# Low parts of the SwiGLU weight operands: a vector subtraction each, or a negation and an accumulating DMA each

## The chip, the cores and the metric

One core of a Trainium2 chip runs the kernel. The metric is device time in microseconds (us). The kernel before took 918.5 us (median of 3 runs, 917.46 to 919.3).

The engines are named as in the profile: PE (TensorE, matrix products; PEld is its loading of weights), DVE (VectorE), ACT (ScalarE), POOL (GpSimd) and SP (SyncE, which here only starts DMAs). Each works through its own queue in order.

## The reference

One layer of an encoder over 768 tokens (512 of a sample, 256 of a prompt), 1024 wide. A mixing block comes first (gated MLP, differential attention, neighbourhood attention), then a layer norm, then SwiGLU, then a layer norm. The change lies in the SwiGLU, whose inner width is 2816:

```python
def swiglu(x, w_gate, w_up, w_down):
    return (jax.nn.silu(x @ w_gate) * (x @ w_up)) @ w_down

def trunk(x, ...):
    ...
        x = layer_norm(DEEPNORM_ALPHA * x + mix, ln_g[l, 0], ln_b[l, 0])
        x = layer_norm(DEEPNORM_ALPHA * x + swiglu(x, w_gate[l], w_up[l], w_down[l]), ln_g[l, 1], ln_b[l, 1])
```

All of it is in float32.

## The kernel before

**Split products.** Every operand of a large product is split into two fp32r parts: `hi` is the value rounded to fp32r, `lo` is what the rounding lost. A product a b is then the sum of hi hi, hi lo and lo hi, three matmuls. Line 113 is the helper: ACT casts (line 114), and then DVE or POOL subtracts (line 115).

```python
def split(hi, lo, src, eng=V):
    S.copy(out=hi, in_=src)
    eng.tensor_tensor(out=lo, in0=src, in1=hi.bitcast(F32), op=ALU.subtract)
```

**The SwiGLU (from about 400 us on).** The inner width is worked through in 11 pairs p of 128-wide feature tiles. A weight of a pair is a 2 x 2 arrangement of blocks, and the block product is taken in seven products instead of eight (Strassen's scheme in Winograd's form), in the order 1, 2, 6, 5, 7, 3, 4. Pair 0 uses eight plain products, and the last two pairs of the down projection use four operands each. Each product has one weight operand of 128 x 512 numbers; there are 219 of them: 8 for pair 0, 140 for gate and up of pairs 1 to 10, 63 for the down projection of pairs 0 to 8, and 8 at the end. A product of gate or up is 12 matmuls 384 columns wide, one of the down projection 9 matmuls 512 columns wide.

For p = 1 to 9 the loop at line 1119 makes seven products of gate, four of the down projection of the pair before, seven of up, and the last three of that down projection: 21 operands. This is called a round below.

**How a weight operand is made.** SP loads a weight subchunk (128 x 1024) into one of 3 `raw` buffers (line 122); an operand group (gate, up or down of a pair) takes two subchunks. Products 1 and 2 use their blocks as loaded. For product 6 POOL forms sums of blocks (line 169), in place of blocks that are no longer needed: a block can be overwritten only when its own split is over. `ws` is one extra buffer for a sum; line 181 fills it again for product 7 of the down projection. Then line 179 splits the operand into a `w` tile; five such tiles hold two operands each, and one is free again when PE has used it. A raw buffer is free for the next load when the last operand made from it has been split: after product 3 (or 5, for the down projection) for the first subchunk of a group and after product 4 for the second.

Line 179 sets who subtracts: POOL for the first 6 operands and for products u3, u4 and d2 later on (`POOL_FIRST`, `POOL_LO`), 34 in all, and DVE for the other 185.

**The other work of a round.** PE's results lie in PSUM banks. ACT copies intermediate sums out (`snap`, line 1018); DVE adds them up (`ffs`, `bv`, line 1023), applies the gate (lines 934 and 937) and adds the down projection into `y` (line 1045). POOL forms sums of the gated blocks (lines 946 to 950), and ACT and DVE split those into `mix`. PE cannot overwrite a bank before DVE or ACT has read it.

**What sets the order.** PE's order is written out by the kernel. The order on ACT, DVE and POOL is worked out by the scheduler of the language from its own timing model; `tc.issue_after` (line 219) only lets the making of new operands in after a given instruction. A DMA that POOL starts stands in POOL's queue like its other instructions.

Of the kernel before, what the change touches and what calls it, by code (L numbers as in the profile page):

```python
# [10 lines left out]
ALU = mybir.AluOpType  # L11
# [3 lines left out]
P = 128  # L15
T = 768          # sample tokens 0..511, prompt tokens 512..767
NS = 512
D = 1024
KT = D // P      # 8
NT = T // P      # 6  # L20
FF = 2816
NFF = FF // P    # 22
# [4 lines left out]
H2 = T // 2      # 384  # L27
NP = NFF // 2    # 11 pairs of feature tiles in the SwiGLU
NP_ST = 9        # pairs whose down projection takes seven block products
PRODUCTS = (1, 2, 6, 5, 7, 3, 4)    # the order of the block products  # L30
OUT_ORDER = [6, 7, 2, 3, 4, 0, 1, 5]    # contraction order of the output projection

# where the smaller parts join the large products, on the clock that these make
CV_LAG = (2.59, 3.84)        # after v of C: its transposes
C_START = 7.75             # attention C: start, period of each pair of heads,
C_PERIOD = (3.18, 6.33)     # stages of a unit in periods
C_AT = (0, 1.03, 1.71, 2.0)
B_START = 61.0            # attention B: the same, and each head's lag after its k
# [3 lines left out]
A_AT = [(7.88, 3.48), (9.39, 3.47), (8.72, 2.82)]    # gMLP: mixing, then transposes  # L42
X1_LAG = (11.34, 9.57, 10.27, 10.2, 8.52, 12.18)    # transposes after the first norm
# how the work of the splits and of the last norm is shared out
POOL_FIRST = 6              # operands of the SwiGLU split with the help of Pool: the first ones,
POOL_LO = ("u3", "u4", "d2")    # and these later on
AHEAD = {"g": 2, "u": 2, "d": 0}    # splits let in by an operand's release
LAST_V = 768                # columns of the last token tile that the vector engine finishes, in two parts
WARM = 8                    # products on zeros before the first ones
LEAD = 2                    # final pieces whose first half runs ahead  # L50
# weight subchunks in the order of use, each [128, 1024]
# [8 lines left out]
def encoder_layer(ctx: ExitStack, tc, a, o):  # L60
# [17 lines left out]
    # The tensor engine keeps the order of emission: `main` holds the large products, whose time  # L78
    # is the clock; everything else is queued on that clock with `later`.
# [23 lines left out]
    # Items 0 .. W_FF - 1 are whole subchunks; from there on an item is a block operand of the  # L103
    # SwiGLU (half a subchunk wide), two of them to a tile.
# [8 lines left out]
    def split(hi, lo, src, eng=V):  # L113
        S.copy(out=hi, in_=src)  # L114
        eng.tensor_tensor(out=lo, in0=src, in1=hi.bitcast(F32), op=ALU.subtract)  # L115

# [26 lines left out]
    def ff_operand(n):  # L143
# [11 lines left out]
        else:  # L155
            if prod == 6:
                # the sums of blocks, in place of blocks no longer needed
                w_sum[key] = s1 = wk2.tile([P, 512], F32, tag="ws", name="ws", bufs=2)
                if down:
                    steps = ((s1, r[0][:, second], r[0][:, first], ALU.subtract),  # L160
                             (r[0][:, first], r[1][:, second], s1, ALU.subtract),
                             (r[1][:, first], r[1][:, first], r[0][:, first], ALU.subtract))
                else:
                    steps = ((s1, r[1][:, first], r[1][:, second], ALU.add),
                             (r[1][:, first], r[0][:, first], r[1][:, first], ALU.subtract),
                             (r[0][:, first], s1, r[0][:, first], ALU.subtract),
                             (r[0][:, second], r[0][:, second], r[0][:, first], ALU.subtract))
                for out, in0, in1, f in steps:
                    G.tensor_tensor(out=out, in0=in0, in1=in1, op=f)  # L169
# [9 lines left out]
        split(op[:, 0], op[:, 1], src, G if n < POOL_FIRST or (n > 16 and key[0] + str(prod) in POOL_LO) else V)  # L179
# [82 lines left out]
    # the tensor engine warms up on zeros while the first loads are under way  # L262
# [64 lines left out]
    # qs[:, m]: the head's own 64 partitions hold q_hi, the other 64 q_lo;  # L327
    # kk[:, m]: k_hi on both halves;  kl: k_lo, head m on its own 64 partitions.
# [52 lines left out]
    for h in range(4):  # L381
# [21 lines left out]
        # sample: first column block, inner column blocks, last column block; prompt: both  # L403
# [8 lines left out]
    def proj_nat(w0, evac):  # L412
        """token-major output, 256 columns: steps of one token tile and two contraction tiles"""
# [19 lines left out]
    def proj_T(wi0, x_hi, x_lo, done):  # L433
        """feature-major output of one 128-wide feature tile, [128, 768]: steps of one contraction tile"""
        st = {}

        def step(k):
            if k == 0:
                st["ps"] = (ps_mm(), ps_mm()[:, :T - NS])
            ps = st["ps"]  # L440
            w = w_tiles[wi0]
            sl = slice(k * P, (k + 1) * P)
            for wi, x in ((0, x_hi), (0, x_lo), (1, x_hi)):
                for p, c0, c1 in ((ps[0], 0, NS), (ps[1], NS, T)):
                    TE.matmul(p, lhsT=w[:, wi, sl], rhs=x[:, k, c0:c1],  # L445
                              start=(k == 0 and wi == 0 and x is x_hi), stop=(k == KT - 1 and wi == 1))
            if k == KT - 1:
                done(ps)
                w_done(wi0)

        return [(0.97, lambda k=k: step(k)) for k in range(KT)]

    def merge(p, q):
        """two lists of steps, evenly mixed"""
# [3 lines left out]
    def chain(stages, at):  # L458
        """stage s of a unit goes at[s] after its start"""
# [6 lines left out]
    def stream(units, period, at, gate=None):  # L466
        """units one period apart; a unit may have to wait for its gate"""
# [20 lines left out]
    cv = mxp.tile([P, NT, 256], F32, tag="mx", name="cv")  # L488

    def c_unit(pr, t):  # L490
# [35 lines left out]
        def values():  # L526
            # out^T, the two heads on their halves of the partitions
# [146 lines left out]
    def a_steps(w0, done):  # L674
        """gelu in stages, for a token tile of u or v"""
        def unit(t, ps):
            u = {}

            def first():
                u["xh"] = xh = wkp.tile([P, 256], F32, tag="xh", name="xh", bufs=2)  # L680
                u["tt"] = tt = wkp.tile([P, 256], F32, tag="tt", name="tt", bufs=2)
                # tanh argument: x * (c + c * 0.044715 * x^2) with x = 2 * xh
# [115 lines left out]
    # x1^T in blocks: 11, 21 the contraction halves of tokens 0..383, 12, 22 those of tokens  # L798
    # 384..767; t1 = 12 - 11, t2 = 22 - t1, t3 = 22 - 12, t4 = 21 - t2.
# [108 lines left out]
    # Products of 2 x 2 blocks take seven block products (Strassen, in Winograd's form): with  # L908
    # s1 = a21 + a22, s2 = s1 - a11, s3 = a11 - a21, s4 = a12 - s2 and t1 .. t4 as above,
    # p1 = a11 b11, p2 = a12 b21, p3 = s4 b22, p4 = a22 t4, p5 = s1 t1, p6 = s2 t2, p7 = s3 t3;  # L910
    # c11 = p1 + p2, c12 = p1 + p6 + p5 + p3, c21 = p1 + p6 + p7 + p4, c22 = p1 + p6 + p7 + p5.
    # One bank gathers p1, p6, p7, p4 and another p2, then p5, p3.
# [18 lines left out]
    def silu(i, src):  # L931
        # silu(x) = x / 2 * (1 + tanh(x / 2))
# [3 lines left out]
    def gated(i, src, p):  # L936
# [4 lines left out]
        # the down projection's blocks: 11, 12 (token, feature halves), their sums, 22  # L941
# [20 lines left out]
    def first_pair():  # L962
        """pair 0 by eight block products: tokens 384 .. 767 come last, their blocks as 11 + t1 and 22"""
        st = {}

        def step(kind, prod, k):
            f, part = prod // 10 - 1, prod % 10      # a f1 b11, a f2 b21, a f1 t1, a f2 b22
# [87 lines left out]
    def piece(i, p):  # L1055
        # part of a token tile, the last two pairs of feature tiles
# [20 lines left out]
    def finish(t, bn):  # L1077
# [4 lines left out]
        # the last steps of the tile before come after the statistics of this one  # L1082
# [60 lines left out]
def _ff_items():  # L1143
    """the weight operands of the SwiGLU in the order of use, and their subchunks in the order of loading"""
# [18 lines left out]
def _layout(inputs):  # L1163
    """Host side: layout only, and constants of the shapes."""
# [8 lines left out]
    def kblocks(w, kt):  # L1173
        # [1024, n] -> subchunks of kt contraction tiles: [128, kt * n]
# [75 lines left out]
```

## Time and profile before

| | |
|---|---|
| median of the runs | 918.5 us (917.46 to 919.3) |
| span of the profiled execution | 916.2 us |
| median of the runs less that span | 2.3 us |
| PE busy | 858.7 us, 94% of the span |
| DVE busy | 702.7 us, 77% |
| ACT busy | 423.2 us, 46% |
| POOL busy | 388.3 us, 42% |

The times of this profile are those of one execution; a run's time also holds a little that lies around the span. Busy shares are means over stages that differ: from 440 us to 820 us DVE is busy some 90% of the time and POOL half of it. A line of the code can be that of a helper: line 115 is every subtraction of a split, so the names of the tiles say which (`w` a weight, `mix` the activations). A wait is put down to what ended it.

### The profile page before, as it was taken

To read this page: it belongs to the slowest core of one execution; us is meant where nothing else is said; L and a number is where in the kernel's file an instruction comes from. 1 tells how busy PE (TensorE), PEld (TensorE's weight loads), DVE (VectorE), ACT (ScalarE), POOL (GpSimd) and SP (SyncE) were. 2 spreads that over 40 slices of the span, in tenths; PEclk is the share of its full clock that TensorE was granted. 3 is DMA by queue.
4 is the path that set the end of the run, shared out by engine and by line. 5 is a ranking of instruction groups with operands and counts; after the bars stand their busy time and mean duration, and the time that the engine had idled before them with its cause. 6 is when DMAs were issued, how large, how long until landed. Compare 5 with 4: busy or idle time off the path is not lost.

```text
span 916.2 us, 13012 instructions
## 1 busy us (share of the span) xinstructions
PE 858.7 (94%) x4811; PEld 761.0 (83%) x4811; DVE 702.7 (77%) x1217; ACT 423.2 (46%) x922; POOL 388.3 (42%) x323
## 2 busy tenths in 40 slices
PE   7999999999999998988999898999899989999995
PEld 6888898888987887887888797888888878879984
DVE  3563437675677569789989898989899898989678
ACT  3474467686665436543434343333334343424422
POOL 0570010100120048885555555554554555653126
PEclk9999999999999999999999999999999999999998
DMA  6830201111017202012222220212222112222223
GB/s 216 246 102 24 69 25 53 40 47 35 15 61 260 70 1 69 23 47 70 69 69 70 69 70 24 92 47 70 69 69 70 69 47 70 69 69 70 70 71 113
DMA packets 22304, 66.66 MB, mean 73 GB/s; under 512 B 3680, under 2 KB 5984, under 8 KB 22240
## 3 DMA queue, kind: packets, MB, share of 16 engines
q1 hardware_dynamic: 22240, 65.82, 21.8%
q8 instruction: 38, 0.62, 0.3%
q14 instruction: 26, 0.21, 0.1%
HBM read 62.67 MB, written 3.15 MB: 72 GB/s over the span
## 4 chain that ended last, share of the span: by engine, by line
PE 50%; DVE 29%; issue 6%; POOL 6%; DMA 5%; ACT 3%; SPq 0%; DVEq 0%; ACTq 0%; POOLq 0%
PE ff L1007 13%; DVE w L115 11%; PE mm L445 9%; PE mm L424 7%; DVE y L1045 6%; PE mm L840 5%; DVE mix L115 5%; PE sc L1040 2%; DVE ffs L934 2%; PE av L608 2%; DMA raw<-in_xT 2%; PE ff L1040 2%; ACT w L114 1%; DMA raw<-in_w 1%; POOL mix L115 1%
## 5 line engine op out<-in xcount | busy, mean ns | idle before, releaser
L115 DVE TENSOR_TENSOR w<-raw,w 128x512 fp32r<-128x512 f32 (+2 forms) x179 | 175.2, 998 | 30.0 <-ACT w L114 29.9
L114 ACT CAST w<-raw 128x512 fp32r<-128x512 f32 (+2 forms) x213 | 137.8, 675 | 105.8 <-PE ff L1007 34.3
L1007 PE MATMUL ff<-x,w 128*128 128x384 f32 x720 | 132.4, 336 | 1.5 <-DVE bv L992 1.5
L1007 PEld LDWEIGHTS ff<-x,w 128*128 128x128 f32 x720 | 126.3, 188 | 3.4 <-DVE bv L992 1.9
L1007 PE MATMUL ff<-xt,w 128*128 128x384 f32 x480 | 90.9, 341 | 13.5 <-DVE ffs L1023 13.5
L1007 PEld LDWEIGHTS ff<-xt,w 128*128 128x128 f32 x480 | 84.6, 190 | 16.4 <-DVE ffs L1023 16.4
L1007 PE MATMUL ff<-mix,w 128*128 128x384 f32 x480 | 92.6, 341 | 3.7 <-DVE bv L1023 2.7
L1007 PEld LDWEIGHTS ff<-mix,w 128*128 128x128 f32 x480 | 86.1, 192 | 5.3 <-DVE bv L1023 4.0
L445 PE MATMUL mm<-xhi,w 128*128 128x512 f32 x320 | 79.1, 346 | 0.5 <-DVE qs L342 0.5
L169 POOL TENSOR_TENSOR ws<-raw 128x512 f32<-128x512 f32 x29 | 41.7, 1440 | 80.4 <-DMA raw<-in_w 66.7
L169 POOL TENSOR_TENSOR raw<-raw 128x512 f32<-128x512 f32 x49 | 70.8, 1446 | 6.8 <-DVE w L115 3.5
L424 PE MATMUL mm<-w,xhi 128*128 128x256 f32 x384 | 71.4, 286 | 0.0
L840 PE MATMUL mm<-w,mix 128*128 128x512 f32 x270 | 68.3, 399 | 1.5 <-ACT tt L684 0.8
L1040 PE MATMUL ff<-w,mix 128*128 128x512 f32 x216 | 59.3, 404 | 10.8 <-DVE y L1045 10.6
L619 POOL TENSOR_TENSOR mn<-mn,neghalf 128x1 f32<-128x1 f32 x24 | 13.7, 572 | 116.2 <-DVE mn L618 112.3
L1018 ACT COPY snap<-ff 128x384 f32<-128x384 f32 x60 | 28.6, 477 | 70.7 <-PE ff L1007 70.7
L840 PEld LDWEIGHTS mm<-w,mix 128*128 128x128 f32 x270 | 49.2, 188 | 12.6 <-ACT tt L684 1.3
L424 PEld LDWEIGHTS mm<-w,xhi 128*128 128x128 f32 x384 | 58.1, 189 | 1.4 <-issue 0.9
L115 POOL TENSOR_TENSOR w<-raw,w 128x512 fp32r<-128x512 f32 x34 | 52.2, 1550 | 16.8 <-ACT w L114 16.6
L1040 PEld LDWEIGHTS ff<-w,mix 128*128 128x128 f32 x216 | 39.1, 189 | 23.8 <-DVE y L1045 17.5
L1040 PE MATMUL sc<-w,mix 128*128 128x512 f32 x189 | 51.8, 407 | 5.0 <-DVE y L1045 5.0
L445 PEld LDWEIGHTS mm<-xhi,w 128*128 128x128 f32 x320 | 49.1, 189 | 6.9 <-issue 0.8
(232 smaller groups left out, 1786.9 us busy)
## 6 DMA issues: line engine op xcount, KB each, us to landing
raw<-in_w SPq DMA_DIRECT2D x95, 512.0 KB, 3.4
y<-in_x SPq DMA_DIRECT2D x6, 512.0 KB, 8.7
raw<-in_xT SPq DMA_DIRECT2D x7, 384.0 KB, 5.0
out_y<-y SPq DMA_DIRECT2D x10, 256.0 KB, 2.0
ln<-in_lng SPq DMA_DIRECT2D x2, 512.0 KB, 6.9
ln<-in_lnb SPq DMA_DIRECT2D x2, 512.0 KB, 8.0
rpb<-in_rpbs SPq DMA_DIRECT2D x32, 30.6 KB, 3.4
rpb<-in_rpbp SPq DMA_DIRECT2D x16, 59.6 KB, 3.0
```

Of the source, the lines that this page charges most:

```text
L114: S.copy(out=hi, in_=src)
L115: eng.tensor_tensor(out=lo, in0=src, in1=hi.bitcast(F32), op=ALU.subtract)
L169: G.tensor_tensor(out=out, in0=in0, in1=in1, op=f)
L424: TE.matmul(ps, lhsT=x[:, k, t * P:(t + 1) * P], rhs=w[:, wi, sl], start=(k == 0 and x is xhi and wi == 0), stop=(k == KT - 1 and x is xlo))
L445: TE.matmul(p, lhsT=w[:, wi, sl], rhs=x[:, k, c0:c1], start=(k == 0 and wi == 0 and x is x_hi), stop=(k == KT - 1 and wi == 1))
L608: TE.matmul(av, lhsT=pT[:, b * P:(b + 1) * P], rhs=vt[:, j0 + b, c0:c0 + P], start=(b == 0), stop=(b == nb - 1))
L840: TE.matmul(ps, lhsT=mix[OUT_ORDER[i]][:, m, t * P:(t + 1) * P], rhs=w[:, wi, sl], start=(i == first and m == 0 and wi == 0), stop=(i == l ...
L934: V.scalar_tensor_tensor(out=TH[i], in0=TT, scalar=1.0, in1=src, op0=ALU.add, op1=ALU.mult)
L1007: TE.matmul(b, lhsT=w[:, wi, k * P:(k + 1) * P], rhs=x1_block(x_name[prod], m, k), start=(prod in (1, 2, 5) and k == 0 and wi == 0 and m = ...
L1018: S.copy(out=t, in_=st[2 if prod == 5 else 1])
L1040: TE.matmul(b, lhsT=gt_block(a_slot[prod], m)[:, t * P:(t + 1) * P], rhs=w[:, wi], start=(prod in (1, 2, 5) and m == 0 and wi == 0), stop= ...
L1045: V.tensor_tensor(out=y[t + dt][:, c], in0=b, in1=y[t + dt][:, c], op=ALU.add)
```

## The change

A second helper makes the split of the SwiGLU's weight operands, and line 179 (of before) calls it:

```diff
+    def split_w(hi, lo, src):
+
+        S.copy(out=hi, in_=src)
+        S.activation(out=lo, in_=src, func=AF.Copy, scale=-1.0)
+        G.dma_start(out=lo, in_=src, accum_op=ALU.add)
...
-        split(op[:, 0], op[:, 1], src, G if n < POOL_FIRST or (n > 16 and key[0] + str(prod) in POOL_LO) else V)
+        split_w(op[:, 0], op[:, 1], src)
```

For each of the 219 operands ACT writes the rounded value to `hi` and the negated rounded value to `lo`; then a DMA started from POOL's queue reads `src` (256 KB) and adds it onto `lo`. The subtraction on DVE or POOL is gone. All other splits (x, the weights of the first stages, `mix`) stay with `split`. The rest of the diff removes comments and doc strings. The new lines shift later line numbers by 6 (line 1045 becomes 1051).

The order of PE and of SP is the same in both kernels. ACT, DVE and POOL change. On POOL, the start of the weights of one round (`L169` and `L181` are the sums of blocks, `w<-raw` a subtraction of a split; from 600.30 us on in the trace), before:

```order
L169 TENSOR_TENSOR raw<-raw,ws 128x512
L115 TENSOR_TENSOR w<-raw,w 128x512
L169 TENSOR_TENSOR raw<-raw 128x512
L181 TENSOR_TENSOR ws<-raw 128x512
L169 TENSOR_TENSOR ws<-raw 128x512
L169 TENSOR_TENSOR raw<-raw 128x512
L169 TENSOR_TENSOR raw<-ws,raw 128x512
```

On POOL at the same place in the changed kernel (its lines 175 and 187 are lines 169 and 181 of before; `L121 DMA` starts an accumulating DMA):

```order
L175 TENSOR_TENSOR raw<-raw,ws 128x512
L121 DMA w<-raw 128x512
L121 DMA w<-ws 128x512
L121 DMA w<-raw 128x512
L175 TENSOR_TENSOR raw<-raw 128x512
L121 DMA w<-raw 128x512
L187 TENSOR_TENSOR ws<-raw 128x512
L121 DMA w<-raw 128x512
L175 TENSOR_TENSOR ws<-raw 128x512
L175 TENSOR_TENSOR raw<-raw 128x512
L121 DMA w<-ws 128x512
L175 TENSOR_TENSOR raw<-ws,raw 128x512
```

The sums of blocks keep their order; between the same sums now stand six starts of DMAs, where one subtraction stood. A sum that writes to `raw` or `ws` waits for the DMA that still reads the old block.

On DVE in the same round, where the gate's last sum is read out and the down projection begins (from 611.12 us on), before:

```order
L1023 TENSOR_TENSOR ffs<-ff,snap 128x384
L115 TENSOR_TENSOR w<-ws,w 128x512
L934 SCALAR_TENSOR_TENSOR ffs<-ffs 128x384
L115 TENSOR_TENSOR w<-raw,w 128x512
L934 SCALAR_TENSOR_TENSOR ffs<-ffs,ff 128x384
L1045 TENSOR_TENSOR y_3122<-ff,y_3122 128x512
L115 TENSOR_TENSOR w<-raw,w 128x512
L1045 TENSOR_TENSOR y_3123<-ff,y_3123 128x512
```

On DVE at the same place in the changed kernel:

```order
L1029 TENSOR_TENSOR ffs<-ff,snap 128x384 x2
L940 SCALAR_TENSOR_TENSOR ffs<-ffs 128x384 x2
L1051 TENSOR_TENSOR y_3122<-ff,y_3122 128x512
L940 SCALAR_TENSOR_TENSOR ffs<-ffs,ff 128x384
L1051 TENSOR_TENSOR y_3123<-ff,y_3123 128x512
```

The three subtractions of weights that stood among the reads of PSUM are gone, so the reads stand directly behind one another.

## Rows read from the trace of the kernel before

**Rows 1.** Busy us by engine (in brackets: instructions): one round, then seven rounds.

```profile
core 0: us, PE busy (x) PEld busy (x) DVE busy (x) ACT busy (x) POOL busy (x), PEclk, DMA share, GB/s
640.59:689.88 49.29, 44.95 (x225) 40.70 (x225) 44.25 (x60) 19.42 (x38) 26.64 (x20) 0.97 0.21 64
444.61:787.12 342.51, 316.45 (x1611) 287.04 (x1610) 308.65 (x420) 137.72 (x266) 188.64 (x134) 0.99 0.20 65
```

**Rows 2.** Waits of PE from 420 us to the end: us, times, longest.

```profile
PE ff L1007 <- DVE ffs L1023: 11.8, 8, 2.6
PE ff L1040 <- DVE y L1045: 10.6, 10, 2.5
PE sc L1040 <- DVE y L1045: 5.0, 9, 0.9
PE ff L1007 <- DVE bv L1023: 2.7, 4, 0.7
```

**Rows 3.** Timeline of POOL, line 946, once a round: start us, us.

```profile
444.61 1.01 POOL L946 TENSOR_TENSOR gs<-bv 128x384 f32<-128x384 f32 x1 [2.76 <-DVE bv L937]
...
787.12 1.40 POOL L946 TENSOR_TENSOR gs<-bv 128x384 f32<-128x384 f32 x1 [2.75 <-DVE bv L937]
```

**Rows 4.** Timeline of PE: start us, us, matmuls; in brackets idle before.

```profile
619.83 0.96 PE L1040 MATMUL ff<-w,mix 128*128 128x512 f32 x3 [2.51 <-DVE y L1045]
...
624.93 4.33 PE L1007 MATMUL ff<-x,w 128*128 128x384 f32 x24
629.10 4.32 PE L1007 MATMUL ff<-xt,w 128*128 128x384 f32 x24
...
665.33 1.54 PE L1040 MATMUL ff<-w,mix 128*128 128x512 f32 x6
666.71 1.53 PE L1040 MATMUL sc<-w,mix 128*128 128x512 f32 x6
```

**Rows 5.** Timeline of DVE before that wait of PE.

```profile
614.22 1.24 DVE L115 TENSOR_TENSOR w<-ws,w 128x512 fp32r<-128x512 f32 x1 [2.54 <-ACT w L114]
615.38 1.65 DVE L934 SCALAR_TENSOR_TENSOR ffs<-ffs 128x384 f32<-128x384 f32 x1
616.95 1.76 DVE L115 TENSOR_TENSOR w<-raw,w 128x512 fp32r<-128x512 f32 x1
618.63 0.54 DVE L934 SCALAR_TENSOR_TENSOR ffs<-ffs,ff 128x384 f32<-128x384 f32 x1
619.10 0.68 DVE L1045 TENSOR_TENSOR y<-ff,y 128x512 f32<-128x512 f32 x1
```

**Rows 6.** Groups in the round 640.59 to 689.88 us: busy us, mean ns | idle before.

```profile
L115 DVE TENSOR_TENSOR w<-raw,w 128x512 fp32r<-128x512 f32 x14 | 11.7, 856 | 0.0
L114 ACT CAST w<-raw 128x512 fp32r<-128x512 f32 x17 | 9.9, 619 | 11.9 <-PE av L1040 4.5 <-PE ff L1007 4.2 <-POOL raw L169 3.2
...
L115 POOL TENSOR_TENSOR w<-raw,w 128x512 fp32r<-128x512 f32 x3 | 4.4, 1481 | 2.8 <-ACT w L114 2.8
L169 POOL TENSOR_TENSOR ws<-raw 128x512 f32<-128x512 f32 x3 | 4.3, 1442 | 7.8 <-DMA raw<-in_w 7.8
L115 DVE TENSOR_TENSOR w<-ws,w 128x512 fp32r<-128x512 f32 x4 | 4.2, 1047 | 0.2 <-ACT w L114 0.2
...
L169 POOL TENSOR_TENSOR raw<-raw,ws 128x512 f32<-128x512 f32 x1 | 1.3, 1293 | 4.0 <-DVE w L115 4.0
```

**Rows 7.** Issues of the weight loads on SP: duration ns min/median/max.

```profile
L122 SPq DMA_DIRECT2D raw<-in_w x95: 327/328/350, 7.0 to 859.2; - x95
```

**Rows 8.** Groups on POOL, whole span, by form: busy us, mean ns | idle before.

```profile
L181 POOL TENSOR_TENSOR ws<-raw 128x512 f32<-128x512 f32 x9 | 15.1, 1681 | 11.2 <-DVE w L115 11.2
...
L401 POOL TENSOR_TENSOR cb<-rpb,mask 128x256 f32<-128x256 f32 x16 | 14.9, 952 | 0.4
```

**Rows 9.** DMA issues by line: KB each, median us from issue to landing.

```profile
raw<-in_w SPq DMA_DIRECT2D x95, 512.0 KB, 3.4
y<-in_x SPq DMA_DIRECT2D x6, 512.0 KB, 8.7
...
out_y<-y SPq DMA_DIRECT2D x10, 256.0 KB, 2.0
```

## The prediction

> **What bounds the kernel now.** I read the busy times by engine first, then PE's waits, then one round of the SwiGLU. Outside the SwiGLU the change touches nothing, so the question is what a round costs.
>
> Seven rounds lie between the first and the last row of [rows 3]: 787.12 - 444.61 = 342.5 us, 48.9 us a round. In them PE is busy 316.45 us of 342.51, DVE 308.65, POOL 188.64 and ACT 137.72 [rows 1]. PE sets the pace, with DVE close behind. PE's waits [rows 2] all name DVE, none the making of weights: 11.8 + 10.6 + 5.0 + 2.7 = 30.1 us from 420 us on. What such a wait is made of can be seen at 619.83 us, where PE stood 2.51 us for an addition into `y` [rows 4]: that addition (619.10 us) stood in DVE's queue behind two subtractions of weights, the first of which had itself waited 2.54 us for its cast [rows 5].
>
> How short a round could be on PE: 24 matmuls of gate or up take 629.10 - 624.93 = 4.17 us, so a product 2.085 us and the 14 of a round 29.2 us; six of the down projection take 666.71 - 665.33 = 1.38 us, 0.23 us each, the 63 of a round 14.5 us [rows 4]. Together 43.7 us. A round thus holds 48.9 - 43.7 = 5.2 us of waiting and of slower matmuls (the granted clock was 0.97 in the round of [rows 1]). This is the most that relief of DVE can give.
>
> **What goes.** Per round DVE loses 14 + 4 subtractions, 11.7 + 4.2 = 15.9 us [rows 6]. Its load falls from 44.25 to 28.4 us of 49.29 [rows 1]. POOL loses three, 4.4 us, and keeps 26.64 - 4.4 = 22.2 us.
>
> **What comes on ACT.** 21 negations. The trace has no such instruction; I price it as the cast of the same tile, 0.62 us [rows 6], with 0.5 and 0.95 us (a POOL pass over half a tile [rows 8]) as ends. ACT goes from 19.4 to 19.4 + 21 x 0.62 = 32.4 us a round; it stays below PE at either end (29.9 to 39.4 us). Queued behind a negation are the `snap` copies that PE needs; at 0.62 us each I cost that at nothing, since PE has one other product (2.085 us) between a bank's end and its next use.
>
> **What comes on POOL.** 21 starts of DMAs a round. No DMA is started from POOL in this trace. The nearest rows: SP starts one in 0.33 us [rows 7], POOL's slowest pass over a whole operand takes 1.68 us and one over half of it 0.95 us [rows 8]. POOL would have to write out 128 rows for each DMA, so SP's price is a floor; I take 1.0 us, next to the half pass and in the middle of the ends. POOL's work per round is then 22.2 + 21 = 43.2 us (29.1 at the low end, 57.5 at the high one).
>
> The Trainium skill, "DMA: Bandwidth & Descriptors", section "Latency and other measured facts", puts the first byte of a POOL-started DMA at about 1 us against 0.6 us for one from SP. By that page POOL's work would be the same 43 us, if the microsecond is all POOL's own; its section "Anatomy of one DMA" calls the generation of descriptors small, by which the low end would hold. No row decides between them.
>
> **What comes as waiting.** A subtraction's result was there when DVE was done, 0.86 us in the mean [rows 6]. An accumulation is there when its DMA has landed. Bounds: 256 KB to memory land in 2.0 us, 512 KB from memory in 3.4 us, and the slowest loads of 512 KB took 8.7 us [rows 9]. The new DMA reads two times 256 KB and writes 256 KB; I take 3.0 us, between the first two, with 2.0 and 8.7 us as ends.
>
> The same wait stands on two paths. One is POOL's queue: a sum that overwrites a block waits until the DMA that reads it has landed. At the start of a round's weights a sum stands only two DMA starts behind the DMA it must wait for (the order above), so about 1 us of 3 remains; the others stand further back. The other is the ring of three raw buffers: a load can start only when the buffer's last operand has landed, and POOL's first sum of a group already waits for loads today, 7.8 us in this round [rows 6]. Three releases a round lie one behind the other on that ring (gate, down, up), and each gets later by 0.62 + 1.0 + 3.0 - 0.86 = 3.8 us: 11.3 us a round. What covers this now is the five `w` tiles: ACT's casts waited 4.5 + 4.2 = 8.7 us in the round for PE to free one [rows 6]. So by the ring a round grows by 11.3 - 8.7 = 2.6 us, before POOL's queue is counted.
>
> By POOL's queue: 43.2 us of work, the 7.8 us for loads that stay, and 3.0 us for one landing in all, 54.0 us a round, 5.1 us over today's 48.9. The two paths overlap; I take the longer one. What is late next is then PE: from a wait for DVE it turns to a wait for weights, behind POOL.
>
> **The sum.** 9 rounds x 5.1 = 46 us. At the end eight operands of the last down products, and at the start eight for pair 0, have little work beside them; a later landing at each costs about 3.0 - 0.86 = 2.1 us, 4 us together. The profiled span is 916.2 us, 2.3 us under the median of the runs. 916.2 + 50 = 966 us as a span, 968 us as a run. This one's own range is 925 to 1010 us (4 more or less a round).
>
> **A page that speaks against the change.** The DMA engines were busy 0.21 of a round, for six loads of 512 KB [rows 1]. If the share goes with bytes read, 21 accumulations of 2 x 256 KB add 3.5 x 0.21 = 0.74, together 0.95; if with bytes written, 0.37, together 0.58. By the first, loads and accumulations would queue behind one another, and a landing could come near the 8.7 us of [rows 9], which the second rival below prices at 1096 us; by the second the forecast stands. The Trainium skill, "Collectives: The Full Stack", section "The bandwidth ceiling", says that an add in a DMA engine halves the rate since it reads two sources in one queue, which is the first reckoning. No row here shows an accumulating DMA.
>
> **The rivals.**
>
> *DVE's relief wins* (chance 0.25). For it: all of PE's waits in the SwiGLU name DVE [rows 2], DVE sheds a third of its round, and POOL was idle 49.29 - 26.64 = 22.7 us of it [rows 1]. At 0.33 us a start POOL has 29.1 us of work and the weights come in time. PE then gets back half of its 5.2 us (DVE's reads still follow its matmuls one by one): 9 x 2.6 = 23 us, 895 us; all of it would give 872 us. Against it: it needs a start below about 0.75 us, by 22.2 + 21 x 0.75 + 7.8 + 3.0 = 48.8 us, the round of today. That is the point from which it decides.
>
> *POOL or the DMA engines bind outright* (chance 0.25). A start at 1.68 us makes POOL 57.5 us + 7.8 + 3.0 = 68.3 us a round, 9 x 19.4 = 175 us more, 1093 us; at 1.3 us it is 60.3 us, 1021 us. A landing of 8.7 us would put the three releases of the ring 17 us later than in the forecast, 9 x (2.6 + 17.1) = 177 us, 1096 us. For it: the floor is SP's, which does no work of its own for the rows; against it, POOL's half pass at 0.95 us.
>
> *It cancels* (chance 0.05): POOL ends at today's round and PE's gain goes into new waits, 918 us.
>
> *The change does not do what it says*: the order above shows POOL with the DMA starts and DVE without the subtractions, so I give this nothing.
>
> **How the numbers follow.** The forecast has 0.45, its rivals 0.25, 0.25 and 0.05. The time is the forecast's, 968 us. The range runs from 890 us (the winning rival's middle and a little below) to 1085 us, just short of the far end of the binding rival; about one in ten lies beyond either end. A measurement of this kernel tells 0.2% (1.8 us) from no change. Slower: 0.45 + 0.25 = 0.70; faster 0.25; the same 0.05.
>
> **What would show it.** Right: POOL's DMA starts near 1 us each, rounds of 53 to 55 us between line 952's instructions (line 946 of before), PE waiting on `w` behind DMAs or ACT instead of on `y` and `ffs`, DVE near 30 us a round, ACT near 32. Wrong: rounds under 49 us, with POOL idle 10 us or more in each (starts are cheap); or landings far above 3 us with the DMA share near 1, where the size would be off and the place with it.

## The result and the profile after

| | before | after |
|---|---|---|
| median of the runs | 918.1 us (917.46 to 919.3, 4 runs) | 999.8 us (997.4 to 1004.54, 4 runs) |
| span of the profiled execution | 916.2 us | 999.8 us |
| PE busy | 858.7 us | 880.4 us, 88% of the span |
| DVE busy | 702.7 us | 553.8 us, 55% |
| ACT busy | 423.2 us | 533.2 us, 53% |
| POOL busy | 388.3 us | 497.1 us, 50% |

The ratio after to before is 1.0899 (95% interval 1.0866 to 1.0931): 82 us slower, where 50 were forecast.

**A round.** Line 952 on POOL, which stands once in a round, gives its length as it did in [rows 3] (start us, us):

```profile
453.06 1.91 POOL L952 TENSOR_TENSOR gs<-bv 128x384 f32<-128x384 f32 x1
...
852.51 1.63 POOL L952 TENSOR_TENSOR gs<-bv 128x384 f32<-128x384 f32 x1
```

852.51 - 453.06 = 399.45 us for seven rounds, 57.1 us each against 48.9. Nine rounds of 8.2 us more are 74 us of the 82. The same round as in [rows 1], seven rounds, and two short stretches inside the first of these, with the columns of [rows 1] (PEclk and DMA share are the third and second last):

```profile
625.89:684.45 58.56, 49.13 (x245) 45.12 (x244) 28.48 (x45) 30.86 (x61) 39.50 (x39) 0.91 0.72 147
453.06:852.51 399.45, 329.93 (x1603) 303.67 (x1602) 203.32 (x292) 210.43 (x412) 265.51 (x260) 0.91 0.75 152
...
670.35:674.50 4.15, 4.15 (x13) 4.15 (x14) 0.00 (x0) 0.80 (x3) 0.86 (x1) 0.51 0.90 225
674.50:682.50 8.00, 8.00 (x48) 8.00 (x47) 3.05 (x4) 4.07 (x8) 6.70 (x6) 1.00 0.60 130
```

Over seven rounds the time grew by 56.9 us. PE's idle time grew from 342.51 - 316.45 = 26.1 to 399.45 - 329.93 = 69.5 us, 43.4 of it. The other 13.5 us are PE's own: its matmuls took longer, since the granted clock was 0.91 in place of 0.99. Where that comes from can be seen in PE's timeline (start us, us, matmuls; in brackets idle before and its end):

```profile
657.37 4.36 PE L1013 MATMUL ff<-x,w 128*128 128x384 f32 x24
662.50 0.62 PE L1013 MATMUL ff<-xt,w 128*128 128x384 f32 x2 [0.77 <-ACT snap L1024]
670.35 5.96 PE L1013 MATMUL ff<-xt,w 128*128 128x384 f32 x22 [7.23 <-DMA w<-raw]
676.15 2.24 PE L1013 MATMUL ff<-mix,w 128*128 128x384 f32 x12
```

PE stood 7.23 us for a landing. The granted clock of the next 4.15 us was 0.51, which is the level of 1.2 GHz: 13 matmuls began in them, where 24 took 4.36 us before the wait. Then it was 1.00 again (2.4 GHz).

**Who is waited for.** PE's waits from 420 us on (us, times, longest) against [rows 2]:

```profile
PE ff L1013 <- ACT snap L1024: 58.9, 21, 6.7
PE ff L1013 <- DMA w<-raw: 23.8, 5, 7.2
PE ff L1013 <- DVE ffs L1029: 3.5, 3, 1.5
PE ff L1046 <- DVE y L1051: 3.3, 2, 2.1
```

The waits for DVE fell from 30.1 to 6.8 us, so the relief is there. Most of the new ones name `snap`, a copy on ACT. ACT's timeline shows what such a copy waits behind:

```profile
614.61 0.62 ACT L119 CAST w<-raw 128x512 fp32r<-128x512 f32 x1 [8.76 <-DMA raw<-in_w]
...
616.70 0.49 ACT L114 CAST mix<-bv 128x384 fp32r<-128x384 f32 x1
617.10 0.84 ACT L1024 COPY snap<-ff 128x384 f32<-128x384 f32 x2
```

The cast of a new weight stood 8.76 us for its load, and the copies behind it in ACT's queue stood with it. The chain of waits of that stretch, and of the one before PE's 7.23 us, names what came before the load (start us, us):

```profile
601.63 4.78 DMA w<-raw
...
606.55 7.96 DMA raw<-in_w
...
614.61 0.18 ACT w L119
...
631.54 4.12 DMA w<-raw
635.80 4.75 DMA raw<-in_w
...
662.54 7.77 DMA w<-raw
...
670.35 12.20 PE ff L1013 x58
```

An accumulation lands, only then does the load into the same raw buffer start, only then can ACT cast. That is the ring of three raw buffers. SP's waits before its loads over the SwiGLU (us, times, longest) name what they waited for, in the kernel before and in the changed one:

```profile
SPq L122 <- DVE w L115: 368.5, 45, 12.5
...
SPq L128 <- DMA w<-raw: 496.5, 57, 21.3
```

Over the SwiGLU the makers of weights waited for loads as follows (before: POOL 64.9 us, ACT none):

```profile
ACT w L119 <- DMA raw<-in_w: 77.3, 24, 9.6
```

```profile
POOL ws L175 <- DMA raw<-in_w: 69.7, 17, 6.6
...
POOL raw L175 <- DMA raw<-in_w: 22.3, 6, 5.2
...
POOL raw L175 <- DMA w<-raw: 4.1, 3, 2.6
```

The waits for loads make 169.3 us together. The last row is a wait that the forecast charged to POOL's queue, a sum held up by a landing: 4.1 us. Two smaller rows add 3.5 us (line 187, which fills `ws` again) and 0.8 us, so it is 8.4 us in all, seven times.

**Sizes.** The groups of the round 625.89 to 684.45 us (columns of [rows 6]):

```profile
L121 POOL DMA_DIRECT2D w<-raw x18 | 19.3, 1362 | 6.6 <-issue 6.4
L120 ACT ACTIVATE w<-raw 128x512 fp32r<-128x512 f32 x18 | 11.3, 629 | 0.0
```

The DMA queues and the DMA issues of the page (share of 16 engines; KB each and median us to landing), against [rows 9]:

```profile
q0 software_dynamic: 31536, 57.42, 34.3%
...
raw<-in_w SPq DMA_DIRECT2D x95, 512.0 KB, 4.4
w<-raw POOLq DMA_DIRECT2D x181, 256.0 KB, 4.7
w<-ws POOLq DMA_DIRECT2D x38, 256.0 KB, 3.6
```

34.3% of 999.8 us over 219 accumulations is 1.57 us of all 16 DMA engines for each. That is more than a start takes on POOL (median of the 181: 1.17 us) and more than ACT needs for an operand (0.61 + 0.63 us). So when a group's operands come in a burst, DMAs have to queue. The busy tenths of the DMA engines in 40 slices from 598 to 616 us show such a burst:

```profile
DMA  9400003997999999999999999999999999995177
```

From the eighth slice on they are full for some 13 us. Landings range from 3.3 to 9.4 us (median 4.6), and the loads in between stretch too, from 3.4 to 4.4 us.

### The profile page after: what moved, and what is told of

It is laid out like the page before. It is cut to its first block, busy times and chain, and to the rows that moved or that the text cites. A ratio compares the mean times of both kernels' runs of the same rounds, so it can differ in the third digit from the quotient of the medians.

```text
span 999.8 us, 13489 instructions
## 1 busy us (share of the span) xinstructions
PE 880.4 (88%) x4811; PEld 784.5 (78%) x4811; DVE 553.8 (55%) x1032; ACT 533.2 (53%) x1141; POOL 497.1 (50%) x508
## 3 DMA queue, kind: packets, MB, share of 16 engines
q0 software_dynamic: 31536, 57.42, 34.3%
## 4 chain that ended last, share of the span: by engine, by line
PE 40%; DMA 21%; POOL 18%; issue 12%; ACT 5%; DVE 3%; SPq 0%; POOLq 0%; DVEq 0%; ACTq 0%
DMA raw<-in_w 10%; PE mm L451 9%; DMA w<-raw 8%; PE mm L430 7%; PE ff L1013 6%; POOL raw L175 6%; POOL w L121 6%; PE mm L846 6%; ACT w L120 2%; POOL ws L175 2%; PE av L614 2%; DMA w<-ws 2%; ACT w L119 1%; PE tp L604 1%; PE sc L585 1%
## 5 line engine op out<-in xcount | busy, mean ns | idle before, releaser
L121 POOL DMA_DIRECT2D w<-raw x181 | 189.6, 1257 | 84.4 <-ACT w L120 67.1
L119 ACT CAST w<-raw 128x512 fp32r<-128x512 f32 x181 | 110.8, 612 | 122.1 <-DMA raw<-in_w 84.0
L1013 PE MATMUL ff<-xt,w 128*128 128x384 f32 x480 | 105.5, 379 | 49.2 <-DMA w<-raw 23.8
L1013 PEld LDWEIGHTS ff<-xt,w 128*128 128x128 f32 x480 | 97.5, 218 | 55.5 <-DMA w<-raw 25.8
L1013 PE MATMUL ff<-mix,w 128*128 128x384 f32 x480 | 100.7, 362 | 33.5 <-ACT snap L1024 33.5
L120 ACT ACTIVATE w<-raw 128x512 fp32r<-128x512 f32 x181 | 113.4, 627 | 0.0
L115 DVE TENSOR_TENSOR mix<-bv,mix 128x384 fp32r<-128x384 f32 x62 | 59.5, 973 | 78.9 <-ACT mix L114 78.7
L1029 DVE TENSOR_TENSOR bv<-ff,snap 128x384 f32<-128x384 f32 x30 | 16.7, 556 | 111.4 <-PE ff L1013 75.3
L694 POOL TENSOR_TENSOR tt<-tt,xh 128x256 f32<-128x256 f32 x12 | 10.1, 840 | 95.2 <-ACT tt L691 95.2
L119 ACT CAST w<-ws 128x512 fp32r<-128x512 f32 x38 | 23.4, 617 | 63.5 <-POOL ws L175 58.3
```

Source lines behind the costliest of these rows:

```text
L120: S.activation(out=lo, in_=src, func=AF.Copy, scale=-1.0)
L121: G.dma_start(out=lo, in_=src, accum_op=ALU.add)
L1013: TE.matmul(b, lhsT=w[:, wi, k * P:(k + 1) * P], rhs=x1_block(x_name[prod], m, k), start=(prod in (1, 2, 5) and k == 0 and wi == 0 and m = ...
L1029: w_state["after"] = V.tensor_tensor(out=out[i], in0=st[b], in1=st["s", other], op=ALU.add).ins
```

## The experiments

Theory R: what costs is the ring, that is, a raw buffer is held until the accumulations that read it have landed, and landings are long. Rivals: starts on POOL (P), load of the DMA engines by itself (D), ACT's negation and the `snap` copies queued behind casts (A). Each edit is to the changed kernel. A kernel without an interval was run once, and single runs can lie some us apart (the four of the changed kernel: 7.1 us). The kernel before took 923.0 us (1 run) beside e_src, e_dveadd, e_plain and e_reldve, 919.5 us (median of 13) beside e_reldma, e_snapdve, e_two and e_few, and 918.8 us (median of 7) beside e_half, e_eighth and e_few2. In the traces of e_src, e_plain, e_half and e_eighth PE and SP keep the order of the changed kernel; ACT, DVE and POOL keep it throughout only in e_plain, and differ in places in the other three.

**e_src: the DMAs stay, but do not read the raw buffers**

```diff
-        G.dma_start(out=lo, in_=src, accum_op=ALU.add)
+        G.dma_start(out=lo, in_=src if w_state["item"] < W_FF + 16 else still[0], accum_op=ALU.add)
```

`still` is a tile that nobody overwrites.

> The changed kernel with one thing altered: from the 17th operand on, the accumulating DMA reads a block of the activations that no longer changes (256 KB, same shape) instead of the raw buffer, so the low parts hold wrong numbers. Number, size, kind and start of the DMAs stay; only the raw buffer is free once ACT has negated, without waiting for the landing. Ring theory (the raw buffers come free only at the landing, and the next load starts only then): a round falls from 57.1 to 50 us or less, the run from 1000 to 920 to 940 us. POOL queue theory (21 starts and 16 sums a round in one queue): still 57 us a round, 990 to 1005 us. DMA load theory (engines 0.72 busy, so everything lands late): still 57 us, 990 to 1005 us. ACT theory (13 us of negations a round hold up the copies that PE waits for): still 57 us.

Measured: 933.4 us, a round of 50.5 us. The median landing was 6.0 us, longer than in the changed kernel, and the DMA share from 440 to 850 us was 0.84 against 0.75. So neither slow landings nor full DMA engines cost the 82 us alone (against D). With the raw buffers free after the negation, the makers' waits for loads fell from 169.3 us to 7.1 + 30.8 + 0.6 = 38.5 us. So 66 of the 82 us are gone. The 10 us that remain over the kernel before are not all that the rest costs, since DVE's relief is in them: against e_plain (below) they are 31 us. PE's largest wait here is one for DVE:

```profile
PE ff L1015 <- DVE ffs L1031: 29.6, 8, 5.7
```

DVE's `mix` subtractions took 1.54 us in the mean over seven rounds, against 1.05 us in the changed kernel. Why they stretch was not tested.

**e_dveadd: the addition on DVE, ACT's negation kept**

```diff
+        V.tensor_tensor(out=lo, in0=src, in1=lo.bitcast(F32), op=ALU.add)
```

(in the place of the DMA)

> The changed kernel with the accumulating DMA replaced by an addition on DVE (lo = lo + src); ACT still casts and negates. All 219 are on DVE, none on POOL. ACT theory: ACT carries the same 32 us a round as in the changed kernel, so most of the loss stays: 980 to 1000 us. Ring, POOL queue and DMA load theories: the loss goes, 915 to 935 us (a little over the kernel before, since DVE also has the 34 subtractions that POOL had).

Measured: 920.0 us. The 219 negations on ACT cost nothing there (against the first half of A).

**e_plain: a plain copy in place of the accumulation**

```diff
+        G.dma_start(out=lo, in_=src)
```

> The changed kernel with a plain copying DMA in place of the accumulating one (lo then holds the source rounded, not the low part). The order on every engine is the same as in the changed kernel, and so is the number of DMA starts. DMA load theory: the share of the DMA engines falls from 0.72 to about 0.45 (one source read instead of two), landings fall from 4.6 to about 3 us, and the run to 950 to 965 us. Ring theory: the same direction, 3 links a round shorter by 1.5 us each plus faster loads, 950 to 975 us. POOL queue theory and ACT theory: 995 to 1005 us.

Measured: 902.3 us, a round of 46.7 us. This is below every forecast (950 us at the least): none of them names DVE's relief as a gain. Its order on every engine is that of the changed kernel, and so are its buffers; only the kind of DMA differs, and with it 97.5 us. Both the landing and the start on POOL are shorter, so this run alone does not tell the two apart. Its page:

```profile
q0 software_dynamic: 31536, 57.42, 20.7%
...
raw<-in_w SPq DMA_DIRECT2D x95, 512.0 KB, 3.9
w<-raw POOLq DMA_DIRECT2D x181, 256.0 KB, 2.6
w<-ws POOLq DMA_DIRECT2D x38, 256.0 KB, 2.4
```

A plain copy of the same 256 KB keeps the 16 engines for 20.7% of 900.5 us / 219 = 0.85 us, lands in 2.6 us, and starts on POOL in 0.53 us. The accumulation's 1.57 us is 1.84 times as much.

**e_reldve and e_reldma: the split divided between the two ways.** `done` holds for the 66 operands that end a raw buffer; e_reldma has `if not done`.

```diff
+        if done:
+            split(op[:, 0], op[:, 1], src, G if ... else V)
+        else:
+            split_w(op[:, 0], op[:, 1], src)
```

> The changed kernel with one third of the operands split as before: those after which a raw buffer is released (products 3 and 4 of gate and up, 5 and 4 of down, blocks 12 and 22 of the plain ones; 66 of 219) are cast on ACT and subtracted on DVE or POOL; the other 153 keep the accumulating DMA. Ring theory: the releases no longer wait for a landing, 925 to 950 us. Theories by amount (POOL queue, DMA load, ACT): the loss shrinks with the count, 82 x 153 / 219 = 57 us over before, about 975 us.

> The kernel before, with the accumulating DMA only for the 66 operands after which a raw buffer is released (the complement of the run in which those 66 were subtracted, 943 us); the other 153 are split as before. Ring theory: each release still waits for a landing, though a shorter one (3.3 to 3.6 us, DMA engines 0.35 busy), so a third of the DMAs brings half of the loss or more, 950 to 970 us. Theories by amount: 82 x 66 / 219 = 25 us over before, about 943 us, or less since DVE is relieved of a third of its subtractions.

Measured: 943.4 us with 153 accumulations on the other operands, and 925.8 us with 66 on those that end a buffer. The narrow form of R, that the releasing operands alone carry the cost, was wrong: they cost 6 us when they are alone (hardly more than single runs lie apart), the others 20. The 925.8 us are where the theories by amount had them (943 us or less). The two parts make 27 us, both together 82.

The premise that e_reldve's releases wait for no landing is wrong too. A raw buffer is free only when every DMA that reads it has landed, not just that of its last operand. SP's waits before its loads from 420 us on still end at a landing 53 times, against 57 in the changed kernel:

```profile
SPq L128 <- DMA w<-raw: 419.9, 53, 15.2
SPq L128 <- DVE w L115: 19.4, 11, 5.5
```

In e_reldma they do so 48 times. So the pair does not part releasing operands from the others. What differs is the landing: 3.4 us (median) with 66 accumulations, 4.0 with 153, 4.6 with 219. In e_reldve POOL's sums wait for landings as well, but for little (us, times, longest):

```profile
POOL raw L175 <- DMA w<-raw: 11.1, 11, 2.1
```

**e_snapdve: the `snap` copies on DVE**

```diff
-        S.copy(out=t, in_=st[2 if prod == 5 else 1])
+        V.tensor_copy(out=t, in_=st[2 if prod == 5 else 1])
```

> The changed kernel with the snap copies, which PE's waits name (58.9 us in all), made on DVE instead of ACT. DVE is idle half of a round. If the copies were late because they stood behind casts in ACT's queue, and that alone cost the time: PE's waits on them go and the run falls by 40 us or more, to 940 to 960 us. Ring theory (the weights are late, and the copies only pass that on): PE's waits move to the weights' DMAs, and the run stays at 985 to 1003 us.

Measured: 1004.7 us, a round of 57.1 us as before the edit. PE's waits changed their names and kept their size:

```profile
PE ff L1013 <- DMA w<-raw: 43.2, 9, 7.8
PE ff L1013 <- DVE snap L1024: 32.9, 12, 6.8
```

The copies only passed the wait on (against the second half of A). The largest line of PE's waits was not the cause.

**e_half and e_eighth: 256 or 64 of the 512 columns**

```diff
-        G.dma_start(out=lo, in_=src, accum_op=ALU.add)
+        G.dma_start(out=lo[:, :256], in_=src[:, :256], accum_op=ALU.add)
```

(`:64` in e_eighth)

> The changed kernel with the accumulating DMA over the first 256 of an operand's 512 columns only (128 KB; the other half of the low part stays the negated high part). As many starts on POOL, as many negations, the same waits; half the time on the DMA engines (1.57 us for each 256 KB in the changed kernel, so about 0.8 us). If the loss comes from landings that stack up behind one another in the DMA engines (1.57 us each, while POOL starts one every 1.2 us and ACT negates one every 1.05 us): most of it goes, 900 to 930 us. If it comes from POOL's starts (1.2 us each) or from ACT: 980 to 1005 us.

> The same over 64 of 512 columns (32 KB). The DMA engines have hardly anything to do for it, and landings are near their floor. Stacked landings: 890 to 910 us, a little below the run with plain copies (902 us). POOL's starts or ACT: 975 to 1005 us. If a start gets shorter with the bytes, its length in the trace says so.

Measured: 939.8 and 912.9 us, 10 and 3 us above the forecasts for stacked landings and far below the others. The start on POOL did not shrink with the bytes: in e_eighth it is 1.10 us in the median, and POOL is busy 323.6 of the 410 us from 440 us on. Yet that kernel is faster than before. So the starts on POOL are not what binds (against P). Against e_plain, whose starts are half as long, e_eighth is 912.9 - 902.3 = 10.6 us slower; what part of that the starts cost was not told apart. The landings' median goes 4.7, 3.4, 2.9 us and the time 999.8, 939.8, 912.9 us.

**e_two: two plain copies in place of one accumulation**, the second from `hi` to a scratch tensor in memory, to double the DMA load.

```diff
+        G.dma_start(out=lo, in_=src)
+        G.dma_start(out=scratch[...], in_=hi.bitcast(F32))
```

> The run with plain copies in place of the accumulations (902 us, landings of 2.6 us, 0.53 us a start), with a second plain DMA behind each that copies the operand's high part (256 KB) to a scratch area in memory. So POOL starts two DMAs of 0.53 us, as much of its time as one accumulating DMA took in the changed kernel (1.17 us), and the DMA engines move the bytes that an accumulation reads; but what releases the raw buffer is still a short plain landing. If the accumulation's price is its late landing in the chain of raw buffers: 900 to 925 us. If it is the load on POOL and on the DMA engines: 970 to 1000 us.

Measured: 1051.7 us, beyond both forecasts, but this tells nothing on the DMA load. POOL's timeline shows why:

```profile
660.60 0.54 POOL L123 DMA_DIRECT2D scratch<-w  x1 [6.63 <-ACT w L119]
661.15 1.30 POOL L177 TENSOR_TENSOR raw<-raw,ws 128x512 f32<-128x512 f32 x1
```

The start of the second copy stood in POOL's queue for a cast, with the sums behind it; such waits add up to 96.6 us. The edit added a wait of its own.

**e_few and e_few2: accumulations on fewer operands, chosen so as to hold nothing up.** e_few uses them for products 6, 5, 7 of gate and up and 6, 7 of down (78), e_few2 for 5, 7 and 7 (49); the rest is split as before.

```diff
+        if prod in ((7,) if down else (5, 7)):
+            split_w(op[:, 0], op[:, 1], src)
+        else:
+            split(op[:, 0], op[:, 1], src, G if ... else V)
```

> A try for a kernel that beats both: the accumulating DMA only for operands that neither are the last of a raw buffer nor read a block that a sum overwrites later: products 6, 5, 7 of gate and up, 6 and 7 of down (78 of 219); the others as before. By the ring theory none of these landings holds up a load, and DVE loses 7 of 18 subtractions a round: 895 to 915 us. If the load on POOL and the DMA engines counts: 920 to 945 us.

> A second try for a kernel that beats both: the accumulating DMA for products 5 and 7 of gate and up and 7 of down only (49 of 219, against 78 in the first try, 914.8 us). DVE is relieved of 4 subtractions a round instead of 7, and ACT has 5 negations instead of 8. If what is left in the first try is PE's waits behind ACT's negations (11.7 us in all): 908 to 914 us. If it is DVE's load: 914 to 919 us.

Measured: e_few 914.8 us (912.12 to 919.67, 10 runs), ratio to before 0.9961 (0.994 to 0.9981). e_few2 **900.6 us** (898.29 to 902.79, 4 runs), ratio 0.9812 (0.979 to 0.9834): it beats both kernels. Its page, and its windows row of seven rounds:

```profile
raw<-in_w SPq DMA_DIRECT2D x95, 512.0 KB, 3.4
w<-ws POOLq DMA_DIRECT2D x29, 256.0 KB, 3.4
w<-raw POOLq DMA_DIRECT2D x20, 256.0 KB, 3.9
```

```profile
441.53:769.68 328.15, 313.79 (x1624) 288.82 (x1624) 283.90 (x386) 157.47 (x302) 215.29 (x169) 0.99 0.38 96
```

Loads are back at 3.4 us, the clock is at 0.99, and a round takes 328.15 / 7 = 46.9 us. These 49 read `ws` or a block that no sum overwrites, and none is the last operand of its raw buffer. e_few2 lies below both of its forecasts (908 us at the least). The operands of both were chosen to hold up no load, but SP's waits before its loads (e_few, then e_few2) still end at a landing 43 and 16 times:

```profile
SPq L128 <- DMA w<-raw: 340.1, 43, 17.1
...
SPq L128 <- DMA w<-raw: 87.5, 16, 13.6
```

That is in line with the 14 us between the two, but they also differ in the number of subtractions and negations, so the cause of these 14 us is not shown.

## Why the prediction was right, and where it fell short

*Direction, and the time within the range: right.* Slower was the likeliest case, and it was slower because a raw buffer is now free only when the DMAs that read it have landed (e_src). That 999.8 us lies inside the range is in part luck: the sum went by a path that did not bind, and a round took 57.1 us where 53 to 55 were to show it right.

*What goes: right.* DVE was busy 28.48 us in the round (28.4 forecast) and its waits fell. The relief is worth about what the winning rival said where the DMA is cheap: e_plain 902 us, that rival 895.

*ACT: right.* A negation takes 0.629 us (0.62 by its price), ACT 30.9 us in a round (32.4).

*POOL's start: right in size.* 1.17 us in the median, 0.85 at the least (1.0 forecast). POOL was busy 39.5 us in the round, less than the 43.2 forecast, since its next instruction often begins before the row of a start has ended.

*The landing: the term that was mis-sized.* I put 3.0 us, between 2.0 and 8.7. It is 3.3 us at the least, 4.7 in the median for blocks from raw buffers, 9.4 at the most. The loads also lengthened, from 3.4 to 4.4 us, which the sum had at nothing.

*The path: the step that failed.* I priced two paths, took POOL's queue (+5.1 us a round) as the longer, and left the ring at +2.6. POOL was less busy than I had it, and its sums waited for landings 8.4 us in all, 0.9 a round where 3.0 were in the sum. What bound was the ring. Its cover was used up, as the forecast had it: from 420 us on ACT's casts waited for PE to free a `w` tile 39.2 + 20.3 + 19.1 = 78.6 us before and 3.1 + 2.5 = 5.6 us after. The ring's own formula, with measured values, gives 0.63 + 1.17 + 4.7 - 0.86 = 5.6 us for a release and 1.0 us for the load after it, 6.6 in all; three a round less the cover of 8.7 us make 11.2 us. The same formula for the kernels that differ only in the DMA:

| kernel | start, landing, load (median us) | ring formula a round | measured a round | difference |
|---|---|---|---|---|
| after | 1.17, 4.7, 4.4 | +11.2 | +8.2 | -3.0 |
| e_half | 1.16, 3.4, 3.8 | +5.5 | +1.7 | -3.8 |
| e_eighth | 1.10, 2.9, 3.5 | +2.9 | -0.5 | -3.4 |
| e_plain | 0.53, 2.6, 3.9 | +1.5 | -2.2 | -3.7 |

The difference hardly moves, and it is near the 2.6 us that the winning rival gave for DVE's relief, which all four kernels have. By this the forecast's ring was the right mechanism with too short a landing, and the relief that I gave to a rival should have been a term of the same sum. The formula was fitted after the runs, to four kernels in which every operand's DMA reads its raw buffer or `ws`. For e_src, whose releases wait for no DMA, it gives less than nothing, and its 10 us are other waits. To e_reldve, where part of the readers are DMAs, it does not apply as it stands.

*`snap` copies at nothing: wrong as to what PE would name, right as to cause.* PE's waits name them for 58.9 us; moved to DVE they left the time where it was.

*The DMA load.* The rows show 0.72 to 0.75 of the DMA engines in use, between the two reckonings (0.95 and 0.58 of a 48.9 us round, which are 0.81 and 0.50 of a 57.1 us one), nearer the first. Against the plain copy the accumulation costs 1.84 times as much engine time. The Trainium skill, "Collectives: The Full Stack", section "The bandwidth ceiling", gives the two source reads as the reason why an add runs at half the rate; these rows agree in size, and show no more of the reason.

*The other rivals.* A landing of 8.7 us for all, or a start of 1.68 us, did not come about: single instances are as long, the medians are not. That the change does nothing falls with the rows.

*Open.* Why DVE's passes stretch in e_src was not tested. That bursts queue in the DMA engines is shown by the full slices and by the landings shrinking with the bytes. How the 55 us beyond the two parts (27 of 82) divide between longer landings and the two kinds of waits locking together was not told apart, since e_two brought a wait of its own. A fourth raw buffer, which would test the ring itself, was not tried.

## What to carry to other kernels

Moving an elementwise pass from a busy engine to a DMA swaps a short time of work for a long time of holding: count for how long the source buffer is now held, and add that to the ring of buffers it belongs to, once for each release in a loop, before counting the issuing engine's time. Use such DMAs for the operands whose source nobody is waiting to reuse, and for few at a time, so that they don't queue: here 49 of 219 gave 1.9% where all of them cost 9% (which of the two did more was not told apart). Count every reader of a buffer, not only the last: one DMA among them is enough to hold it until that DMA has landed. The engine named by the largest waits may only pass a wait on; follow the chain back until a buffer's release begins it.

## What the runs showed of the hardware

- The start of an accumulating DMA on POOL has a row of 0.85 us at the least and 1.17 us in the median, that of a plain one 0.53 us. A transfer of an eighth of the bytes takes nearly as long to start (1.10 us).
- 256 KB accumulated within the core's memory landed in 3.3 us at the least and 4.6 us in the median of the changed kernel, plain copies of e_plain in 2.2 and 2.6 us; they used the 16 DMA engines for 1.57 against 0.85 us.
- After a wait of PE of 7.23 us the granted clock was 0.51 for the next 4.15 us. Over seven rounds the slower matmuls made 13.5 of 56.9 us, a cost that no wait shows.
- A subtraction `mix<-bv,mix` of 128x384 on DVE took 0.54 us at the least in the kernel before, the changed one and e_src; the longest took 1.65, 4.0 and 5.6 us. The additions `y<-ff,y`, which read PSUM, stayed between 0.67 and 0.69 us in the changed kernel and e_src. What stretches the first was not tested.
